# A list schedule that reaches from layer A to the last out projection, taken in passes from both ends

## The chip, the cores and the metric

The kernel runs on one core of a Trainium2 chip. The metric is the device time of one execution in microseconds (us), as the median over repeated executions. The profile and the trace come from one further execution on the hardware. Engines are named as the profile names them: PE (matmuls), PEld (its weight loads), DVE (vector), ACT (scalar), POOL (GpSimd) and SP, whose queue issues every DMA of this kernel.

## What is computed

One inference step of two layers, for a prompt of 1024 tokens and 8 samples of 8 tokens each (64 further columns), at width 1024. The reference, cut to what matters:

```python
def short_conv_mixer(u, buf, w_in, w_conv, w_out):          # layer A
    p = u @ w_in                                            # 1024 -> 4096
    y, new_buf = causal_dwconv(c_gate * h, buf, w_conv)
    return (b_gate * y * jax.nn.silu(z)) @ w_out, new_buf

def gdn_mixer(u, conv_buf, s0, w_in, w_conv, ...):          # layer B, 8 heads of 128
    p = u @ w_in                                            # 1024 -> 4112
    qkv, new_buf = causal_dwconv(p[..., :3072], conv_buf, w_conv)
    ...
    o, S = gated_delta_rule(q, k, v, g, beta, s0)           # triangular solve per chunk, scan over chunks
    o = o * lax.rsqrt(jnp.mean(o * o, ...) + NORM_EPS) * norm_w
    return (o * jax.nn.silu(z)) @ w_out, new_buf, S

for l in range(2):
    u = x * (1.0 + scale) + shift                           # shift, scale, gate = silu(c) @ w_mod + b_mod
    out, ... = mixer(u, ...)
    x = layer_norm(ALPHA * x + gate * out, ln_g[l], ln_b[l])
```

Activations and weights are float32.

## The kernel before

**Layer A.** The input of the layer is held as two fp32r tiles per column group, `uh` (rounded) and `ul` (the rest), in three groups of 384, 384 and 320 columns; every weight block is split the same way into `wh` and `wl` (ACT rounds, DVE subtracts). A product is three matmuls per 128 rows of k: `wh*uh`, `wh*ul`, `wl*uh` (`mm_k`). `chan_a(j)` computes channel block j from four such products; it ends with a multiplication on POOL and a store to the scratch tensor `d_y[0]`. Beside channels 1 and 2 the second layer's modulation (`mod_gate`, `mod_cols`, matmuls against `csT`) is computed, beside channels 3 to 7 the out-projection weights are split (`load_wo`).

**Out projection of a layer** (`out_proj`). Nine tiles of 128 tokens (the ninth has the 64 sample rows). Per tile: reload `y` from scratch and split it (`load_y`), 48 matmuls of 512 columns into two PSUM banks (`mm`), then `norm`: gate and residual on DVE, `bn_stats`, a square root on ACT, a Newton step on DVE, and `finish`. In layer A `finish_a` normalizes on ACT (`xt`), multiplies `x1` by the layer norm's vectors on POOL (two instructions of 1024 columns), transposes `xt` on PE into the bank `t1`, and forms `uh` and `ul` of layer B. In layer B `finish_b` ends in the store of `y`.

**Layer B.** 32 products of the same kind as in layer A (three per head and the gates `z`), and beside them per head and half a chain: `prep` (transposes, Gram products, then a triangular inverse by levels in fp16, tiles `AH`, `DH`, `EH`, `YH`, `id16`), `scan` (fp32 matmuls of 128 columns, `S` to `S`), and `norm_out`. `sample(p)` does the same for the samples of two heads; its last part updates the sample states `S0` (load, scale on ACT, one matmul of 512 columns, add on DVE, store). `out_weights` loads and splits layer B's out-projection weights into the space of `uh` and `ul` once the last products have read it.

**What sets the order.** Every instruction goes through `Clock`, which hands it to `Plan.add`. While `Plan.on` is true, `Plan` records it with a price (`Plan.price`: busy time, and the time until it is seen) and with the instructions that it depends on. `Plan.arrange` is a list scheduler: each of five queues (T is PE, V is DVE, A is ACT, G is POOL, D is SP's DMAs) takes, when it is free, the ready unit with the highest rank, and the order found is tied to the program by dependencies that cost no wait. Outside of it instructions stand as they are written. In the kernel before `Plan.on` is set ahead of `gates` (the start of layer B) and `arrange` is called behind the last chain, ahead of layer B's out projection; the rank is the longest way to the end of that stretch.

Of the kernel before, what the change touches and what calls it, by code (L numbers as in the profile page):

```python
# [8 lines left out]
F32R = mybir.dt.float32r  # L9
F16 = mybir.dt.float16  # L10
# [105 lines left out]
class Plan:  # L116
# [2 lines left out]


    CELL = 128
    on = False

    @classmethod
# [26 lines left out]
        return t  # L151


    V = ((1, 0.155), (128, 0.345), (256, 0.41), (512, 0.69), (1112, 1.34))
    G = ((1, 0.25), (128, 0.4), (512, 1.3), (1112, 2.65))

    @staticmethod
    def along(table, n):
# [5 lines left out]
    @classmethod  # L164
    def price(cls, kind, name, outs, ins, args, kw):
        n = outs[0].free_size()
        if kind == "T":
            x = kw["rhs"] if "rhs" in kw else None
            if x is None:
                return max(0.055, outs[0].free_size() * 0.00083 + 0.0025), 0.2  # L170
            n, cols = x.free_size(), kw["lhsT"].free_size()
            if x.dtype == F32R:
                return n * 0.0004475 + 0.0025, 0.2
            if x.dtype == F32:
                return max(0.222 if cols > 64 else 0.0, n * (2 / 1200.0 if cols > 32 else 0.5 / 1200.0) + 0.005), 0.2
            return max(0.029, n / 2400.0 + 0.0023), 0.2
        if kind == "D":
            return 0.06, 2.0 + min(x.free_size() for x in outs + ins) * P * 4 / 3e5
        if kind == "V":
            wide = [x for x in outs + ins if x.free_size() > 1]  # L180
            if len(wide) > 1 and all(x.dtype == F16 for x in wide):
                n = n / 2
            return cls.along(cls.V, n) - 0.08, 0.115
        if kind == "G":
            t = 1.02 if ALU.pow in args else cls.along(cls.G, n) * (1.0 if len(ins) > 1 else 0.5)
            return t - 0.06, 0.1
        t = 0.2 + 0.00066 * n if ins[0].space == PSUM else 0.18 + 0.0009 * n
        t += 0.2 * ("accum_out" in kw) + 0.11 * hasattr(kw.get("scale"), "free_size")
        return t - 0.1, 0.135


# [14 lines left out]
    @classmethod  # L206
    def add(cls, kind, name, outs, ins, args, kw, inst):
        if not cls.on:
            return
        i = len(cls.nodes)  # L210
        deps, behind = set(), set()
        bank = {x.name for x in (*ins, *outs) if x.space == PSUM}
        for x in bank:

            if x in cls.writer:
                j = cls.writer[x]
                (behind if cls.nodes[j][0] == kind else deps).add(j)
            cls.writer[x] = i
        rc = {c for x in ins if x.name not in bank for c in cls.cells(x)}
        wc = {c for x in outs if x.name not in bank for c in cls.cells(x)}  # L220
        for c in rc | wc:
            if c in cls.writer:
                deps.add(cls.writer[c])
        for c in wc:
            deps |= cls.readers.pop(c, set())
            cls.writer[c] = i
        for c in rc:
            cls.readers.setdefault(c, set()).add(i)
        for x in (*outs, *ins):
# [12 lines left out]
        if kind == "T":  # L242
            x = kw.get("rhs", kw.get("in_"))
            wide = x.dtype == F32R
            if cls.unit and cls.unit[1] == outs[0].name and not (wide and cls.unit[2] >= 3) and max(deps, default=0) < cls.unit[0]:
                unit = cls.unit[0]
                cls.unit[2] += 1
            else:
                cls.unit = [i, outs[0].name, 1]
        else:  # L250
            wide = False
            if cls.unit and any(x.name == cls.unit[1] for x in (*outs, *ins)):
                cls.unit = None
        func = args[2] if kind == "A" and len(args) > 2 else None
        table = {AF.Exp: 1, AF.Silu: 2, AF.Sqrt: 3}.get(func, 0)
        cls.nodes.append((kind, inst, unit, deps, *cls.price(kind, name, outs, ins, args, kw), wide, table, behind, [x.name for x in outs]))


    @classmethod
    def arrange(cls, tc):  # L260
        import heapq

        cls.on = False

        def order(i, j):
            tc.add_manual_dep(i, j.name, mybir.DependencyInfo(mybir.DependencyClass.NoSync, mybir.DependencyReason.DATA), reason="order")

        nodes = cls.nodes
# [1 line left out]
        for i, v in enumerate(nodes):  # L270
            units.setdefault(v[2], []).append(i)

            old = [d for x in v[9] for y in cls.before.get(x, ()) for d in cls.users.get(y, ())]
            deps.setdefault(v[2], set()).update(nodes[d][2] for d in (*v[3], *old))
            behind.setdefault(v[2], set()).update(nodes[d][2] for d in v[8])
            for d in v[8]:
                if nodes[d][0] != v[0]:
                    order(v[1], nodes[d][1])
        after, follow = ({u: [] for u in units} for _ in range(2))
        for u in units:  # L280
            deps[u].discard(u)
            behind[u] -= deps[u] | {u}
            for d in deps[u]:
                after[d].append(u)
            for d in behind[u]:
                follow[d].append(u)
        cost = {u: (sum(nodes[i][4] for i in units[u]), max(nodes[i][5] for i in units[u])) for u in units}
        left = {u: len(deps[u]) + len(behind[u]) for u in units}
        line = [u for u in units if not left[u]]
        for u in line:  # L290
            for v in after[u] + follow[u]:
                left[v] -= 1
                if not left[v]:
                    line.append(v)
        assert len(line) == len(units)
        way = {}
        for u in reversed(line):
            way[u] = max(sum(cost[u]) + max((way[v] for v in after[u]), default=0.0), max((way[v] for v in follow[u]), default=0.0))
        left = {u: len(deps[u]) + len(behind[u]) for u in units}
        ready = dict.fromkeys(units, 0.0)  # L300
        coming, waiting = ({k: [] for k in "TVAGD"} for _ in range(2))
        free, last = dict.fromkeys("TVAGD", 0.0), dict.fromkeys("TVAGD", None)
        state = {"T": True, "A": 0}
        for u in units:
            if not left[u]:
                heapq.heappush(coming[nodes[u][0]], (0.0, u))
        for _ in units:
            t, k = min((free[k] if waiting[k] else max(free[k], coming[k][0][0]), k) for k in "TVAGD" if waiting[k] or coming[k])
            while coming[k] and coming[k][0][0] <= t:
                u = heapq.heappop(coming[k])[1]  # L310
                heapq.heappush(waiting[k], (-way[u], u))
            u = heapq.heappop(waiting[k])[1]
            busy, seen = cost[u]
            if k == "T":
                wide = nodes[u][6]
                busy += 0.078 * (wide and not state["T"])
                state["T"] = wide
            elif k == "A" and nodes[u][7]:
                busy += 1.28 * (nodes[u][7] != state["A"])
                state["A"] = nodes[u][7]  # L320
            free[k] = t + busy
            for i in units[u]:
                if last[k] is not None:
                    order(nodes[i][1], last[k])
                last[k] = nodes[i][1]
            for v, at in [(v, t + busy + seen) for v in after[u]] + [(v, t) for v in follow[u]]:
                ready[v] = max(ready[v], at)
                left[v] -= 1
                if not left[v]:
                    heapq.heappush(coming[nodes[v][0]], (ready[v], v))  # L330


class Pool:
# [30 lines left out]
def tile_trunk(ctx, tc, I, O):  # L364
# [239 lines left out]
    with ExitStack() as actx:  # L604
# [270 lines left out]
                load_wm(9 + i)  # L875

        extra.extend(lambda i=i: mod_next(i) for i in range(len(mods)))
        load_wm(8)
        chan_a(1)
        chan_a(2)  # L880
# [87 lines left out]
    with ExitStack() as bctx:  # L968
# [15 lines left out]
        gt = ExitStack()  # L984
        gtp = pool_in(gt, "gt", 1)

        Plan.on = True

        def gates():
            cong = gtp.tile([P, const_width("cong")], F32, name="cong")  # L990
# [600 lines left out]
        while chains or filler or fillers or upcoming or todo:  # L1591
# [16 lines left out]
            else:  # L1608
# [3 lines left out]
                except StopIteration:  # L1612
                    filler = None
                drain(1)
        Plan.arrange(tc)
        sB2.close()
        sB.close()

# [11 lines left out]
        with ExitStack() as fctx:  # L1630
# [22 lines left out]

            out_proj(1, wk, (3, 2, 0), wo, gP, gS, finish_b, lns, beside, constants)
            beside(("sampled", 3))


_OUT = (("y_p", (SEQ, D)), ("y_s", (NS, D)), ("ca_p", (P, KT, 2)), ("cb_p", (P, 24, 3)), ("s_p", (H, P, P)),
# [100 lines left out]
```

## Time and profile before

| | |
|---|---|
| Median of 3 runs | 1360.61 us (1359.68 to 1361.13) |
| The profiled execution, own time | 1356.89 us |
| Its span | 1355.1 us |
| PE busy | 1309.0 us, 97% of the span |
| DVE, ACT, POOL busy | 831.9, 652.9, 209.4 us |
| DMA moved | 160.22 MB, 118 GB/s over the span |

The page divides the span into 40 slices and gives each engine's busy share in tenths. Matmuls are pipelined, so a PE that is busy throughout may still start its matmuls further apart than it could. All instructions stand on one line (L106), since `Clock` issues them all; groups are told apart by the tiles they write and read. Layer A runs to about 432 us, its out projection to about 558 us, layer B to about 1250 us, and its out projection to the end.

### The profile page before, as it was taken

Reading aid. Unit: us, or ns where it says so; the run is one execution under the profiler, and the core shown is the slowest. Engines: PE = TensorE matmul, PEld = TensorE weight load, DVE = VectorE, ACT = ScalarE, POOL = GpSimd, SP = SyncE. Lnnn points to the kernel's source line nnn. Section 1 sums busy time; section 2 is a strip of 40 time slices with the busy share of each in tenths; the row PEclk is TensorE's granted clock in tenths of the full one; section 3 lists DMA queues with packets and bytes.
Section 4 is the critical chain, followed back from the end, with each engine's and each line's share of the span. In section 5 each row is a group of like instructions: output and inputs, shape, how many; then the busy total and the mean of one; then the engine's idle time right before and its main releaser. Section 6 shows DMA issues by size and latency. Waiting matters only on the chain.

```text
span 1355.1 us, 27508 instructions
## 1 busy us (share of the span) xinstructions
PE 1309.0 (97%) x10631; PEld 1197.4 (88%) x10631; DVE 831.9 (61%) x2010; ACT 652.9 (48%) x1878; POOL 209.4 (15%) x326
## 2 busy tenths in 40 slices
PE   7999999999999999898999999999999999998997
PEld 5898889999999777798999899999999899996775
DVE  3444143244233688667866877787787667557687
ACT  3411212222221355478965768676776567445321
POOL 0011000000000144211121212130303102001041
PEclk9999999999999999999999999999999999999999
DMA  8735542221212332246331232222222224336852
GB/s 310 265 126 190 223 135 77 87 83 68 86 65 68 123 125 88 73 130 187 118 101 50 67 111 80 67 74 88 67 84 83 89 71 129 113 130 202 252 177 68
DMA packets 119023, 160.22 MB, mean 118 GB/s; under 512 B 21220, under 2 KB 74220, under 8 KB 116844
## 3 DMA queue, kind: packets, MB, share of 16 engines
q1 hardware_dynamic: 118892, 158.46, 36.3%
q8 instruction: 83, 1.36, 0.4%
q14 instruction: 48, 0.39, 0.1%
HBM read 123.61 MB, written 34.82 MB: 117 GB/s over the span
## 4 chain that ended last, share of the span: by engine, by line
PE 44%; DVE 7%; DMA 4%; ACT 2%; issue 1%; POOL 1%; SPq 0%; POOLq 0%; ACTq 0%; DVEq 0%
PE g L106 24%; PE t L106 13%; PE s L106 5%; PE o L106 3%; DVE acc L106 1%; DMA S<-in_s_dram 1%; DVE xt L106 1%; DVE wl L106 1%; DMA E<-d_rows 1%; DMA rb<-d_rows 1%; DMA wr<-in_wb_dram 0%; DMA wr<-d_y 0%; DVE Y L106 0%; POOL f1y L106 0%; DVE st L106 0%
## 5 line engine op out<-in xcount | busy, mean ns | idle before, releaser
L106 PE MATMUL g<-uh,wh 128*128 128x384 f32 (+3 forms) x1080 | 376.2, 352 | 1.1 <-DVE wh L106 0.8
L106 PE MATMUL g<-ul,wh 128*128 128x384 f32 (+3 forms) x1080 | 355.1, 332 | 0.0
L106 PE MATMUL g<-uh,wl 128*128 128x384 f32 (+2 forms) x1064 | 350.6, 333 | 0.2 <-DVE wl L106 0.2
L106 DVE TENSOR_TENSOR wl<-wr,wh 128x256 fp32r<-128x256 f32 (+1 forms) x225 | 133.6, 610 | 178.1 <-ACT wh L106 177.9
L106 ACT ACTIVATE wh<-wr 128x256 fp32r<-128x256 f32 (+2 forms) x227 | 109.3, 501 | 213.6 <-PE t L106 118.1
L106 PEld LDWEIGHTS g<-uh,wh 128*128 128x128 f32 (+1 forms) x1080 | 202.2, 187 | 6.1 <-issue 1.2
L106 PEld LDWEIGHTS g<-ul,wh 128*128 128x128 f32 (+1 forms) x1080 | 202.1, 187 | 2.8
L106 PEld LDWEIGHTS g<-uh,wl 128*128 128x128 f32 x1064 | 199.4, 188 | 2.7 <-DVE wl L106 0.5
L106 PE MATMUL t<-uh,wh 128*128 128x384 f32 (+3 forms) x540 | 177.7, 336 | 4.1 <-ACT uh L106 2.9
L106 PE MATMUL t<-ul,wh 128*128 128x384 f32 (+3 forms) x540 | 177.1, 335 | 0.1
L106 PE MATMUL t<-uh,wl 128*128 128x384 f32 (+2 forms) x532 | 173.7, 333 | 0.3 <-DVE wl L106 0.3
L106 DVE SCALAR_TENSOR_TENSOR acc<-xb,wbc,acc 128x512 f32<-128x512 f32 (+1 forms) x144 | 113.8, 792 | 19.1 <-ACT acc L106 18.5
L106 PEld LDWEIGHTS t<-uh,wh 128*128 128x128 f32 (+1 forms) x540 | 101.4, 188 | 16.0 <-issue 6.3
L106 PEld LDWEIGHTS t<-ul,wh 128*128 128x128 f32 (+1 forms) x540 | 101.8, 188 | 5.1 <-issue 2.1
L106 PEld LDWEIGHTS t<-uh,wl 128*128 128x128 f32 x532 | 100.3, 189 | 3.6 <-issue 0.8
L106 ACT ACTIVATE xb<-g 128x384 f32<-128x384 f32 (+4 forms) x122 | 49.7, 413 | 78.8 <-PE g L106 77.7
L106 ACT ACTIVATE EH<-t 128x256 f16<-128x256 f32 (+1 forms) x176 | 57.0, 365 | 5.4 <-PE t L106 4.7
L106 ACT ACTIVATE DH<-t 128x256 f16<-128x256 f32 (+1 forms) x128 | 46.6, 384 | 23.3 <-PE t L106 22.3
L106 PE MATMUL t<-DH,AH 128*128 128x64 f16 x1176 | 52.3, 193 | 1.5 <-DVE DH L106 0.9
L106 PEld LDWEIGHTS <-AH 128*128 128x128 f16 x1176 | 43.4, 98 | 9.9 <-issue 7.2
L106 PEld LDWEIGHTS <-EH 128*128 128x128 f16 x1120 | 41.9, 98 | 9.6 <-issue 4.3
L106 ACT ACTIVATE YH<-Y 128x256 f16<-128x256 f32 (+1 forms) x104 | 41.7, 402 | 17.1 <-DVE Y L106 15.2
(361 smaller groups left out, 2377.7 us busy)
## 6 DMA issues: line engine op xcount, KB each, us to landing
wm<-in_wm_dram SPq DMA_DIRECT2D x16, 1024.0 KB
wr<-in_wb_dram SPq DMA_DIRECT2D x64, 256.0 KB
wr<-in_wa_dram SPq DMA_DIRECT2D x62, 256.0 KB
wm<-in_wm_dram SPq DMA_DIRECT2D x16, 512.0 KB
wr<-d_y SPq DMA_DIRECT2D x32, 256.0 KB
S<-in_s_dram SPq DMA_DIRECT2D x32, 256.0 KB
d_y<-cs SPq DMA_DIRECT2D x8, 544.0 KB
wr<-in_wo_dram SPq DMA_DIRECT2D x16, 256.0 KB
```

Source lines behind the costliest of these rows:

```text
L106: r = call(*args, **kw)
```

## The change

The list schedule covers everything from channel 1 of layer A to the last instruction: `Plan.on` is set ahead of `load_wm(8)`, and `arrange` is called at the end. The scheduler itself is replaced. `order` is one pass of list scheduling over a graph; `arrange` runs six times forward and, between them, on the reversed graph, and each pass takes its ranks from the start times of the pass before; the forward pass with the smallest modelled end is used. On the PE queue a pass may stay with the kind of matmul that runs (fp16 or not) as long as the best of that kind is within `STAY` of the best of all, and it adds 0.08 when it leaves fp16. Prices change too: short DVE and POOL instructions cost a little more, `bn_stats` has its own price, and DMAs occupy their queue by size and run length instead of 0.06 each. What is computed stays the same, and so does each instruction; only places in the queues change.

```diff
+    STAY = 4.0
+    PASSES = 6
...
-    V = ((1, 0.155), (128, 0.345), (256, 0.41), (512, 0.69), (1112, 1.34))
-    G = ((1, 0.25), (128, 0.4), (512, 1.3), (1112, 2.65))
+    V = ((1, 0.18), (128, 0.345), (256, 0.41), (512, 0.69), (1112, 1.34))
+    G = ((1, 0.3), (128, 0.4), (512, 1.3), (1112, 2.65))
...
         if kind == "D":
-            return 0.06, 2.0 + min(x.free_size() for x in outs + ins) * P * 4 / 3e5
+
+            size = min(x.shape[0] * x.free_size() for x in outs + ins) * 4
+            run = min((x.ap[-1][1] if x.ap[-1][0] == 1 else 1) for x in outs + ins) * 4
+            rate = 340e3 if run >= 2048 else 300e3 if run >= 1024 else 200e3 if run >= 512 else max(8e3, run * 300.0)
+            return max(0.06, size / rate), 2.0
+        if kind == "V" and name == "bn_stats":
+            return 0.05 + 0.00106 * ins[0].free_size(), 0.115
...
-            wide = x.dtype == F32R
-            if cls.unit and cls.unit[1] == outs[0].name and not (wide and cls.unit[2] >= 3) and max(deps, default=0) < cls.unit[0]:
+            wide = 2 if x.dtype == F32R else x.dtype != F16
+            if cls.unit and cls.unit[1] == outs[0].name and not (wide == 2 and cls.unit[2] >= 3) and max(deps, default=0) < cls.unit[0]:
...
+    def order(cls, kinds, cost, edges, rank):
...
+        for _ in cost:
+            t, k = min((free[k] if waiting[k] else max(free[k], coming[k][0][0]), k) for k in "TVAGD" if waiting[k] or coming[k])
+            w = waiting[k]
+            while coming[k] and coming[k][0][0] <= t:
+                u = heapq.heappop(coming[k])[1]
+                heapq.heappush(w, (-rank[u], u))
+            top = w[0]
+            if k == "T":
+                if (kinds[top[1]][1] == 0) != (state[k] == 0):
+                    top = min((x for x in w if (kinds[x[1]][1] == 0) == (state[k] == 0) and x[0] <= top[0] + cls.STAY), default=top)
+                if kinds[top[1]][1] and not state[k]:
+                    t += 0.08
+                state[k] = kinds[top[1]][1]
+            elif k == "A" and kinds[top[1]][2]:
+                t += 1.28 * (kinds[top[1]][2] != state[k])
+                state[k] = kinds[top[1]][2]
...
+            u = top[1]
+            start[u], free[k] = t, t + cost[u][0]
+            queue[k].append(u)
+            for v, lag in edges[u]:
+                ready[v] = max(ready[v], t + lag)
...
+        return max(start[u] + sum(cost[u]) for u in cost), start, queue
...
         for u in reversed(line):
-            way[u] = max(sum(cost[u]) + max((way[v] for v in after[u]), default=0.0), max((way[v] for v in follow[u]), default=0.0))
...
+            rank[u] = max((rank[v] + lag for v, lag in ahead[u]), default=sum(cost[u]))
+        best = None
+        for _ in range(cls.PASSES):
+            r = cls.order(kinds, cost, ahead, rank)
+            if best is None or r[0] < best[0]:
+                best = r
+            start = cls.order(kinds, cost, back, {u: t + cost[u][0] for u, t in r[1].items()})[1]
+            rank = {u: t + cost[u][0] for u, t in start.items()}
+        for queue in best[2].values():
+            line = [i for u in queue for i in units[u]]
+            for i, j in zip(line, line[1:]):
+                tie(nodes[j][1], nodes[i][1])
...
+        Plan.on = True
         load_wm(8)
         chan_a(1)
...
-        Plan.on = True
-
         def gates():
...
-        Plan.arrange(tc)
         sB2.close()
         sB.close()
...
             beside(("sampled", 3))
+            Plan.arrange(tc)
```

Three places show what moves.

PE in layer B, inside `prep` of head 0: `t1` and `t0` are the banks of the two halves' level products, `g` the bank of a product with `uh` and `ul`. Before, the end of one fp16 group of the second half:

```order
L106 MATMUL t1_6282<-id16_76,DH1_5817 128x64
L106 LDWEIGHTS DH1_5817
L106 MATMUL t1_6282<-id16_76,DH1_5817 128x64
L106 LDWEIGHTS DH1_5817
L106 MATMUL t1_6282<-id16_76,DH1_5817 128x64
L106 MATMUL g_6445<-uh2_101,wh_5930 128x320
L106 MATMUL g_6445<-ul2_104,wh_5930 128x320
L106 MATMUL g_6445<-uh2_101,wl_5931 128x320
```

In the change, the end of the same group:

```order
L106 MATMUL t1_6282<-id16_76,DH1_5817 128x64
L106 LDWEIGHTS DH1_5817
L106 MATMUL t1_6282<-id16_76,DH1_5817 128x64
L106 LDWEIGHTS DH1_5817
L106 MATMUL t1_6282<-id16_76,DH1_5817 128x64
L106 LDWEIGHTS AH0_5724
L106 MATMUL t0_6325<-DH0_5725,AH0_5724 128x64
```

The fp16 group of the first half (`t0_6325`), which stood by itself between two pieces of a product before, now follows the second half's group. Over the whole program fp16 matmuls are followed by a matmul of another kind at 236 places before and at 151 places in the change.

PE in layer A's out projection, where the eight transposes of the second token tile (`xt_4003`) stand; its sums are complete with the last matmul into `t0_3857` and `t0_3858`. Before, they stand amid the products of the fourth tile (`g_4119`, `g_4120`):

```order
L106 MATMUL g_4119<-woh3_1800,wl_4007 128x512
L106 MATMUL g_4120<-woh3_1800,wl_4007 128x512
L106 MATMUL g_4119<-woh4_1802,wh_4012 128x512
L106 MATMUL t1_4093<-cons_75,xt_4003 128x128 x4
L106 MATMUL t1_4105<-cons_75,xt_4003 128x128 x4
L106 MATMUL g_4120<-woh4_1802,wh_4012 128x512
L106 MATMUL g_4119<-wol4_1803,wh_4012 128x512
L106 MATMUL g_4120<-wol4_1803,wh_4012 128x512
```

In the change they stand behind the last of them:

```order
L106 MATMUL g_4120<-woh6_1806,wl_4013 128x512
L106 MATMUL g_4120<-woh7_1808,wh_4012 128x512
L106 MATMUL g_4120<-wol7_1809,wh_4012 128x512
L106 MATMUL g_4120<-woh7_1808,wl_4013 128x512
L106 MATMUL t1_4093<-cons_75,xt_4003 128x128 x4
L106 MATMUL t1_4105<-cons_75,xt_4003 128x128 x4
L106 MATMUL t0_4235<-woh0_1794,wh_4170 128x512
L106 MATMUL t0_4235<-wol0_1795,wh_4170 128x512
```

Counted in matmuls from a tile's last product to its transposes: before, 51, 49 and five times 48 of 512 columns for the first seven tiles, and 24 of 512 and 24 of 256 for the eighth; in the change 48 for the first tile, 93, 96, 96 and 96 for the second to the fifth, 72 for the sixth, 72 and 39 of 256 for the seventh, 24 and 48 of 256 for the eighth. Behind the ninth stand 32 matmuls of 384 columns before and 27 in the change. On ACT, the first tile's square root and normalization stand ahead of three roundings (`wh_3972`, `wh_4006`, `wh_4012`) in the change and behind them before.

DVE at the end, behind the last products of the ninth tile's bank `g_17623` (`xt_17589` is the ninth tile, `xt_17497` the eighth, `S0` the last two sample states). Before:

```order
L106 TENSOR_TENSOR tmp_17736<-g_17623,gS_16817 64x256
L106 SCALAR_TENSOR_TENSOR xt_17589<-xt_17589,tmp_17736 64x256
L106 BN_STATS st_17723<-xt_17589 64x6
L106 BN_AGGR mv_17724<-st_17723 64x2
L106 TENSOR_SCALAR ve_17725<-mv_17724 64x1
L106 SCALAR_TENSOR_TENSOR xt_17589<-xt_17589,mv_17724,ln_g_16818 64x896
L106 RECIPROCAL rs_17742<-rt_17743 64x1
```

In the change:

```order
L106 TENSOR_TENSOR tmp_17736<-g_17623,gS_16817 64x256
L106 RECIPROCAL rs_17686<-rt_17687 128x1
L106 TENSOR_TENSOR S0_16944<-S0_16944,t0_16995 128x512
L106 SCALAR_TENSOR_TENSOR xt_17589<-xt_17589,tmp_17736 64x256
L106 TENSOR_TENSOR rt_17687<-rs_17686,ve_17674 128x1
L106 BN_STATS st_17723<-xt_17589 64x6
L106 SCALAR_TENSOR_TENSOR rt_17687<-rt_17687,rs_17686 128x1
L106 TENSOR_TENSOR S0_17014<-S0_17014,t0_17067 128x512
L106 BN_AGGR mv_17724<-st_17723 64x2
L106 SCALAR_TENSOR_TENSOR rs_17686<-rt_17687,rs_17686 128x1
L106 TENSOR_SCALAR ve_17725<-mv_17724 64x1
L106 TENSOR_SCALAR nm_17675<-mv_17673,rs_17686 128x1
```

The two additions into `S0`, whose matmuls are now the last two of the program on PE, and the end of the eighth tile stand between the ninth tile's instructions; before, they came earlier.

## Rows read from the trace of the kernel before

**Rows 1.** The page: busy time by engine.

```profile
PE 1309.0 (97%) x10631; PEld 1197.4 (88%) x10631; DVE 831.9 (61%) x2010; ACT 652.9 (48%) x1878; POOL 209.4 (15%) x326
```

**Rows 2.** Stages: busy us (instructions) of each engine, TensorE clock, DMA share, GB/s.

```profile
core 0: us, PE busy (x) PEld busy (x) DVE busy (x) ACT busy (x) POOL busy (x), PEclk, DMA share, GB/s
55.00:440.00 385.00, 385.00 (x2347) 367.22 (x2344) 136.43 (x293) 78.60 (x136) 25.70 (x36) 1.00 0.33 113
440.00:562.00 122.00, 112.50 (x539) 87.78 (x538) 93.37 (x160) 56.15 (x120) 42.79 (x23) 0.97 0.33 107
562.00:660.00 98.00, 93.65 (x722) 89.44 (x720) 71.80 (x196) 77.46 (x182) 11.72 (x32) 1.00 0.48 146
660.00:1200.00 540.00, 532.85 (x5866) 505.41 (x5866) 395.46 (x1042) 367.25 (x1246) 101.06 (x196) 1.00 0.28 85
1200.00:1355.10 155.10, 138.25 (x865) 112.99 (x863) 111.76 (x259) 51.28 (x147) 27.08 (x30) 0.97 0.56 174
```

**Rows 3.** Who PE waited for, 440 to 562 us: us, times, longest.

```profile
PE t L106 <- ACT xt L106: 7.2, 4, 2.8
PE t L106 <- ACT uh L106: 1.4, 1, 1.4
```

**Rows 4.** The same, 562 to 660 us.

```profile
PE t L106 <- DVE kn L106: 1.0, 1, 1.0
```

**Rows 5.** The same, 660 to 1200 us.

```profile
PE t L106 <- DMA S<-in_s_dram: 2.0, 2, 1.6
```

**Rows 6.** The same, 1200 us to the end.

```profile
PE s L106 <- DVE qg L106: 2.9, 1, 2.9
PE t L106 <- DMA S<-in_s_dram: 1.9, 1, 1.9
PE t L106 <- ACT wh L106: 1.1, 1, 1.1
```

**Rows 7.** Three short stretches, columns as in rows 2.

```profile
496.90:500.20 3.30, 3.30 (x11) 2.71 (x10) 3.30 (x2) 3.28 (x9) 3.22 (x2) 0.50 0.06 16
500.30:503.70 3.40, 3.40 (x16) 2.72 (x16) 3.40 (x4) 0.68 (x2) 1.17 (x1) 1.00 0.45 147
1251.20:1254.60 3.40, 3.40 (x11) 2.75 (x9) 2.08 (x4) 1.91 (x5) 0.00 (x0) 0.50 0.53 171
```

**Rows 8.** Timeline of PE behind a run of fp16 matmuls: start, us.

```profile
803.24 0.42 PE L106 MATMUL g<-uh,wh 128*128 128x384 f32 x1
803.50 0.34 PE L106 MATMUL g<-ul,wh 128*128 128x384 f32 x1
803.67 0.34 PE L106 MATMUL g<-uh,wl 128*128 128x384 f32 x1
```

**Rows 9.** Chain that ended last, two late pieces: start, us, what.

```profile
1312.45 11.04 PE g L106 x48
...
1342.81 2.81 PE g L106 x24
```

**Rows 10.** Timeline of DVE and POOL, 461 to 468 us.

```profile
461.12 0.69 DVE L106 TENSOR_TENSOR wl<-wr,wh 128x512 fp32r<-128x512 f32 x1
466.15 2.20 DVE L106 TENSOR_TENSOR wl<-wr,wh 128x512 fp32r<-128x512 f32 x1
465.39 2.40 POOL L106 TENSOR_TENSOR x<-xt,ln_g 128x1024 f32<-128x1024 f32 x1 [30.62 <-ACT rt L106]
```

**Rows 11.** Timeline of DVE, pieces of the last 100 us.

```profile
1257.90 0.69 DVE L106 TENSOR_TENSOR S<-S,t 128x512 f32<-128x512 f32 x1 [4.14 <-PE t L106]
1340.20 1.01 DVE L106 SCALAR_TENSOR_TENSOR xt<-xt,rs,ln_b 128x768 f32<-128x768 f32 x1
1348.61 0.15 DVE L106 TENSOR_TENSOR rt<-rs,ve 64x1 f32<-64x1 f32 x1
```

**Rows 12.** Timeline of SP and ACT: one load of out-projection weights.

```profile
1239.71 0.34 SPq L106 DMA_DIRECT2D xb<-in_wo_dram  x1
1243.36 1.15 ACT L106 ACTIVATE uh<-xb 128x512 fp32r<-128x512 f32 x2 [0.78 <-DMA xb<-in_wo_dram]
```

More of the change, by code (lines that the diff above doesn't have):

```diff
@@ L187, in price @@
         t = 0.2 + 0.00066 * n if ins[0].space == PSUM else 0.18 + 0.0009 * n
-        t += 0.2 * ("accum_out" in kw) + 0.11 * hasattr(kw.get("scale"), "free_size")
+        t += 0.2 * ("accum_out" in kw) + 0.1 * hasattr(kw.get("scale"), "free_size")
         return t - 0.1, 0.135
@@ L259, in arrange, with tie @@
     @classmethod
+    def order(cls, kinds, cost, edges, rank):
+        import heapq
+        left, ready = dict.fromkeys(cost, 0), dict.fromkeys(cost, 0.0)
+        for u in cost:
+            for v, _ in edges[u]:
+                left[v] += 1
+        coming, waiting = ({k: [] for k in "TVAGD"} for _ in range(2))
+        free, state, queue, start = dict.fromkeys("TVAGD", 0.0), {"T": 2, "A": 0}, {k: [] for k in "TVAGD"}, {}
+        for u in cost:
+            if not left[u]:
+                heapq.heappush(coming[kinds[u][0]], (0.0, u))
+        for _ in cost:
[14 more added lines that the diff above has]
+                state[k] = kinds[top[1]][2]
+            if top is w[0]:
+                heapq.heappop(w)
+            else:
+                w.remove(top)
+                heapq.heapify(w)
+            u = top[1]
[3 more added lines that the diff above has]
+                ready[v] = max(ready[v], t + lag)
+                left[v] -= 1
+                if not left[v]:
+                    heapq.heappush(coming[kinds[v][0]], (ready[v], v))
+        return max(start[u] + sum(cost[u]) for u in cost), start, queue
+    @classmethod
     def arrange(cls, tc):
-        import heapq
         cls.on = False
-        def order(i, j):
+        def tie(i, j):
             tc.add_manual_dep(i, j.name, mybir.DependencyInfo(mybir.DependencyClass.NoSync, mybir.DependencyReason.DATA), reason="order")
@@ L277, in arrange @@
                 if nodes[d][0] != v[0]:
-                    order(v[1], nodes[d][1])
-        after, follow = ({u: [] for u in units} for _ in range(2))
+                    tie(v[1], nodes[d][1])
+        kinds = {u: (nodes[u][0], nodes[u][6], nodes[u][7]) for u in units}
+        cost = {u: (sum(nodes[i][4] for i in units[u]), max(nodes[i][5] for i in units[u])) for u in units}
+        ahead, back = ({u: [] for u in units} for _ in range(2))
         for u in units:
[L281 to L288, printed above, removed]
+            lags = {d: 0.0 for d in behind[u]}
+            lags.update((d, sum(cost[d])) for d in deps[u])
+            lags.pop(u, None)
+            for d, lag in lags.items():
+                ahead[d].append((u, lag))
+                back[u].append((d, cost[u][0] + lag - cost[d][0]))
+        rank = {}
+        left = {u: len(back[u]) for u in units}
         line = [u for u in units if not left[u]]
         for u in line:
-            for v in after[u] + follow[u]:
+            for v, _ in ahead[u]:
                 left[v] -= 1
@@ L295, in arrange @@
         assert len(line) == len(units)
-        way = {}
         for u in reversed(line):
-            way[u] = max(sum(cost[u]) + max((way[v] for v in after[u]), default=0.0), max((way[v] for v in follow[u]), default=0.0))
[L299 to L330, printed above, removed]
```

## The prediction

> **What bounds the kernel now.** I read the busy line of the page first: PE is busy for 97% of the span, DVE for 61%, ACT for 48% [rows 1]. So time can only come from PE: from places where it waits, and from places where it starts its matmuls further apart than it must. Next I cut the span into stages [rows 2]. From 55 to 440 us (layer A's channels) PE is busy in all 385 us, and no row of the waits names it there: the schedule cannot gain in the larger part of the stretch that it newly covers. From 440 to 562 us (layer A's out projection) PE is idle for 122.0 - 112.5 = 9.5 us, from 562 to 660 us (the start of layer B) for 4.4, from 660 to 1200 us for 7.2 of 540, and from 1200 us to the end for 16.9, of which 9.5 lie behind the last matmul, which ends at 1342.81 + 2.81 = 1345.6 [rows 9]. That is 38 us of idle PE in all. Then I read the waits of PE stage by stage: in the out projection the transposes wait four times for the normalized tile, 7.2 us together, and the last gate product 1.4 us for `uh` [rows 3]; at the start of layer B the chain's first steps wait, as for `kn`, 1.0 us at a time [rows 4]; in the body the longest total is 2.0 us for a sample state's load [rows 5]; around 1250 us there are 2.9, 1.9 and 1.1 us [rows 6].
>
> Two further costs do not show as idle time. The granted clock fell from its 2.4 GHz level to 1.2 GHz (0.50 in the rows) in three stretches of some 3.3 us, each right behind a wait of PE: 11 matmuls start in 3.3 us, and 16 in the 3.4 us that follow [rows 7], so each such stretch costs about 5 matmuls of 0.23 us, 1.2 us. And behind a run of fp16 matmuls the next product starts its second matmul after 0.26 us, where the following distance is 0.17 [rows 8]: leaving fp16 costs 0.08 to 0.09 us.
>
> **The change part by part.** Nothing is added or removed; PE's work is the same, so each term is a wait or a change of kind that appears or goes. The sum is made against the profiled span of 1355.1 us; that execution took 1356.89 us, 3.7 below the median of 1360.61, and I carry the difference over to the median.
>
> (a) Fewer exits from fp16. 236 exits become 151: 85 x 0.08 = -6.8 us. This counts in full only where PE is the bound, and in the body it is: 7.2 us idle in 540. Bounds -7.2 and 0 (a chain that now waits for its partner could give it back).
>
> (b) Layer A's out projection. The wait in front of the transposes is what the norm needs, less what stands between. Before, 51 matmuls of 0.23 us [rows 9] stood there and PE still waited 2.8 us, so the first tile's norm took 51 x 0.23 + 2.8 = 14.5 us. Now the second to the seventh tile have at least 72 matmuls, 16.6 us, in between: their waits go. The first has 48 (11.0 us), but its norm goes ahead of three roundings on ACT, 0.6 us each [rows 12], and of the splits on DVE; I expect a wait of 0 to 1.5 us. The eighth had 24 of 512 and 24 of 256 columns, now 24 and 48 (some 11 us in place of 8). The ninth has fewer than before, so the 1.4 us behind it stay. Of 7.2 us I take 5.8 as gone, and of the two slow-clock stretches of this stage the one behind a transposes' wait: 5.8 + 1.2 = -7. Bounds -8.4 and 0.
>
> Here one observation speaks against the change. DVE's split of a tile takes 0.69 us, but 2.20 us when it begins while POOL multiplies `x1` [rows 10]. The Trainium skill says why (SBUF — State Buffer, Who interferes with whom): a DVE instruction with both inputs in SBUF and a GpSimd instruction that reads SBUF take the same read interface, and whichever comes second waits until the other ends. The trace agrees, with 2.20 against 0.69 us. By that rule the planner's prices are wrong here, since they give such a DVE instruction one price whatever POOL does. In the sum it stays out, because the same 18 POOL instructions run in either order; it is the slower rival below.
>
> (c) Start of layer B. The first transposes of `kn`, the first Gram products and the first fp16 steps stand 1 to 5 us of products later than before, which covers waits of 1.0 us each [rows 4]. Idle time was 4.4 us: -2.5. Bounds -4.4 and +2 (the gates' chain decides, and nobody fills more).
>
> (d) Body of layer B. The waits are of eight kinds, none over 2.0 us in total [rows 5]; the new order is made by the same kind of list, so I expect as many in other places: 0, bounds -5 and +6.
>
> (e) Around 1250 us. The chain of the last head and the final sample states met there. Now the products reach about 10 us further into the last scan, and the last sample states are put off to the end, so the waits for `qg` and for the state's load shrink. A new one comes: on SP the load of the second block of out-projection weights stands behind the store of the last head's state, and a load takes 3.65 us from its issue to the rounding that uses it [rows 12]; PE has 18 matmuls of the first block, 4.1 us, to run meanwhile, part of them already behind it; I count 1 to 2 us of wait. Of 5.9 us [rows 6] and one slow-clock stretch of 1.2 us I take -5. Bounds -7.1 and +3.
>
> (f) The end. DVE works off the ninth tile's norm behind the last matmul. Now two additions into the sample states, 0.69 us each, one instruction of 768 columns, 1.01 us, and some six short ones of 0.15 us [rows 11] stand between: 1.4 + 1.0 + 0.9 = +3.3. Bounds 0 and +4.
>
> (g) Layer A's channels: there was no wait, so a new order can only add one. The modulation is done earlier, with its weights loaded closer together. +1, bounds 0 and +3 (one wait of the longest kind in these rows, 2.9).
>
> Sum: -6.8 - 7 - 2.5 + 0 - 5 + 3.3 + 1 = -17. The span becomes 1338, the median 1360.6 - 17 = **1343.6 us**.
>
> **The rivals.**
>
> *Given back in part.* The waits move on instead of going: the first tile still waits, each stage keeps half of its waits, and the fp16 steps, now tied in pairs, wait for the slower half. For it: idle time of PE is small and spread, and ACT is busy for 77.46 us of 98 at the start of layer B [rows 2]. Against it: the distances in the out projection grew from 12 to over 16 us. Then (a) -4, (b) -3.5, (c) and (e) -3 together, (f) and (g) +4.3: -6, about 1354 us.
>
> *No change.* What was gained in the body is lost at the end and in the newly planned channels, or the order of instructions does not do what its model says because DMA decides: within 2.7 us of 1360.6. For it: the end is longer by 3.3 us for sure, and layer A's channels can only lose.
>
> *Slower: DVE is held by POOL in layer A's out projection.* This is the rule named above, as a mechanism of this kernel: a planned DVE order that places instructions with two SBUF inputs under the POOL pair of each tile. DVE is busy for 93.37 of 122 us there [rows 2], with nine tiles 10.4 us a tile; PE needs 48 x 0.23 and the transposes, about 11.9 us a tile. Each further instruction caught costs 2.20 - 0.69 = 1.5 us, so from the second one a tile on, DVE is the bound. With four more, 10.4 + 6.0 - 11.9 = 4.5 us are lost on each of seven tiles, 32 us, and (b) is not earned: -10 + 32 = +22, about 1382 us; with three more, +11. Against it: the POOL pair takes about 5 us a tile, before as now, and PE's transposes now stand a full tile later, so that a late DVE has room first.
>
> **How the numbers follow.** Forecast (-10 to -27 us) 0.60; given back in part (-2.7 to -10) 0.21; no change 0.09; slower 0.10, nearly all of it the POOL mechanism with three or more instructions a tile. A difference of 0.2%, 2.7 us, is about what a measurement of this kernel can tell from none. So faster 0.81, same 0.09, slower 0.10. The range: all best bounds of (a) to (g) together give -32, which is too much to expect; -30 is the low end, 1330. The high end takes in the partial return and the lower half of no change: 1358. Outside remain the slower case and a little on either side.
>
> **What would show it.** In the profile of the changed kernel: of PE's waits between 440 and 562 us the one for `xt` falls from 7.2 to under 2 us, and only one or no slow-clock stretch lies there; between 660 and 1200 us PE's work takes some 7 us less; around 1250 us the wait for `qg` is under 1 us, and a wait for `uh` or `wl` behind a weight load takes its place; behind the last matmul 12 to 13 us pass instead of 9.5, with `S` among DVE's last instructions. The prediction is wrong if layer A's channels show PE idle, if the out projection lasts as long as before with DVE busy throughout, or if the body's waits grow by more than the 6.8 us that the exits give.

## The result, and the profile after

The changed kernel takes 1337.20 us (median of 4 runs, 1334.88 to 1338.62) against 1360.14 us (4 runs) of the kernel before: ratio 0.9831, 95% interval [0.9813, 0.9849], 22.9 us less. On a second chip it again took 1337.19 us, but the kernel before took 1353.79 there: ratio 0.9865 [0.9843, 0.9886], 16.6 us less. The change repeats itself; the kernel before moves by some 6 us from chip to chip. The forecast of 1343.6 us lies 6.4 us above the result and inside its range. The profiled execution has a span of 1335.9 us against 1355.1. So the two traces show 19.2 of the 22.9 us between the medians; the other 3.7 come from which executions were profiled, 3.25 us below its median before (1356.89 us) and 0.4 above it in the change (1337.63).

The busy line of the page, which answers to [rows 1]: the same work, PE still at 97% of a span that is 19.2 us shorter.

```profile
PE 1296.5 (97%) x10631; PEld 1193.8 (89%) x10631; DVE 834.3 (62%) x2010; ACT 656.3 (49%) x1884; POOL 207.3 (16%) x326
```

The stages, columns as in [rows 2]:

```profile
55.00:440.00 385.00, 382.79 (x2345) 365.01 (x2344) 134.70 (x291) 73.23 (x136) 30.01 (x37) 1.00 0.33 110
440.00:562.00 122.00, 115.40 (x550) 90.60 (x549) 97.49 (x167) 57.14 (x124) 42.53 (x22) 0.96 0.37 117
562.00:660.00 98.00, 96.28 (x764) 94.36 (x763) 68.56 (x185) 78.92 (x180) 12.24 (x34) 0.99 0.41 131
660.00:1200.00 540.00, 535.95 (x6056) 512.47 (x6055) 411.74 (x1100) 383.92 (x1296) 96.99 (x200) 1.00 0.30 91
1200.00:1335.90 135.90, 119.59 (x632) 96.60 (x630) 99.09 (x208) 40.93 (x103) 24.51 (x26) 0.97 0.59 187
```

Idle PE is now 2.2 us in layer A's channels (0 before), 6.6 in its out projection (9.5), 1.7 at the start of layer B (4.4), 4.1 in the body (7.2) and 16.3 behind 1200 us (16.9). Whom PE waited for, the same five stretches in order:

```profile
PE g L106 <- DVE xb L106: 1.1, 1, 1.1
PE t L106 <- DVE cs L106: 1.1, 1, 1.1
...
PE s L106 <- ACT wh L106: 3.4, 1, 3.4
PE t L106 <- ACT xt L106: 2.0, 1, 2.0
PE t L106 <- ACT uh L106: 0.6, 1, 0.6
...
PE t L106 <- DVE kn L106: 1.7, 1, 1.7
...
PE t L106 <- DVE DH L106: 1.2, 2, 0.6
PE s L106 <- DVE vn L106: 0.9, 1, 0.9
...
PE s L106 <- DVE wl L106: 2.5, 1, 2.5
PE s L106 <- DVE qg L106: 1.6, 1, 1.6
PE t L106 <- ACT vx L106: 1.4, 1, 1.4
```

Against [rows 3]: `xt` fell from 7.2 us in four waits to one of 2.0 (the ninth tile's), but a wait of 3.4 us for `wh` is new, and the granted clock falls behind both. Columns as in [rows 7]:

```profile
467.60:471.00 3.40, 3.40 (x10) 2.65 (x9) 0.69 (x1) 3.21 (x9) 0.00 (x0) 0.50 0.90 284
471.00:474.40 3.40, 3.40 (x16) 2.73 (x15) 3.06 (x4) 0.95 (x2) 1.68 (x1) 1.00 0.07 29
556.30:563.10 6.80, 5.95 (x24) 4.07 (x24) 3.95 (x9) 3.23 (x9) 2.88 (x9) 0.50 0.25 63
```

The stretch at the 1.2 GHz level near 560 us is 6.8 us long now; before it was about 3.4. These two cost much of the gain in this stage: layer A's last product ends 2.5 us later than before, the out projection's last one 3.3 us earlier, and the last gate product at the same time, 562.2 us.

At the end, pieces of the chain that ended last (start, us, what):

```profile
1320.31 2.80 PE g L106 x24
1323.11 0.25 PE t L106
...
1325.30 0.69 DVE S L106
...
1326.45 0.93 DVE xt L106
...
1327.45 1.46 DVE xt L106
```

The last product ends at 1323.11 us, 22.5 us earlier than in [rows 9]; behind it 12.75 us pass instead of 9.50.

**Where the time came from**, in the two traces, each stage from the end of one's last product to the end of the next. A pause here is more than 0.25 us beyond the usual distance of such matmuls:

| | predicted | measured |
|---|---|---|
| (a) exits from fp16, 236 and 151 | -6.8 | -6.75 (19.25 to 12.5 us) |
| (b) layer A's out projection and gates | -7 | -2.4 |
| (c) to 660 us, pauses | -2.5 | -3.8 (5.75 to 1.9) |
| (d) body, pauses | 0 | -4.75 (10.8 to 6.0) |
| (e) from 1200 us, pauses | -5 | -3.9 (8.8 to 4.95), and some of the next row |
| smaller distances and low clock in (c) to (e) | | -3.3 |
| (f) the end | +3.3 | +3.25 |
| (g) layer A's channels | +1 | +2.5 |
| sum | -17 | -19.2 |

The sum and the ends of stages do not depend on how a pause is counted, the split between the rows does: with the usual distance taken from the matmul in front, (a) is 17.6 to 11.1 us, (c) 5.4 to 1.9, (d) 9.3 to 5.2 and (e) 8.7 to 4.7.

### The profile page after: what moved, and what is told of

Read it like the earlier page. It is cut to its first block, busy times and chain, and to the rows that moved or that the text cites. A ratio compares the mean times of both kernels' runs of the same rounds, so it can differ in the third digit from the quotient of the medians.

```text
span 1335.9 us, 27510 instructions
## 1 busy us (share of the span) xinstructions
PE 1296.5 (97%) x10631; PEld 1193.8 (89%) x10631; DVE 834.3 (62%) x2010; ACT 656.3 (49%) x1884; POOL 207.3 (16%) x326
## 5 line engine op out<-in xcount | busy, mean ns | idle before, releaser
L106 PE MATMUL g<-uh,wh 128*128 128x384 f32 (+3 forms) x1080 | 382.6, 356 | 1.5 <-DVE xb L106 1.1
L106 DVE TENSOR_TENSOR wl<-wr,wh 128x256 fp32r<-128x256 f32 (+1 forms) x225 | 139.0, 630 | 59.3 <-ACT wh L106 58.9
L106 DVE COPY bias<-t 128x1 f32<-128x1 f32 x29 | 4.6, 157 | 148.2 <-PE t L106 148.2
L106 DVE TENSOR_TENSOR Y<-t,cons 128x256 f32<-128x256 f32 (+1 forms) x104 | 41.5, 404 | 21.1 <-PE t L106 20.7
```

The source lines that it names most:

```text
L106: r = call(*args, **kw)
```

## The experiments

All ratios are to the kernel before on the same chip; "the change" is 0.9831 or 0.9865 by chip, as above.

| run | us | ratio, 95% interval |
|---|---|---|
| e1_new_list_old_stretch | 1340.09 | 0.9885 [0.9866, 0.9904] |
| e2_old_list_new_stretch | 1377.33 | 1.0158 [1.0137, 1.0179] |
| e3_no_stay | 1341.64 | 0.9897 [0.9878, 0.9916] |
| e4_one_pass | 1340.36 | 0.9890 [0.9871, 0.9910] |
| e5_change_again | 1337.19 | 0.9865 [0.9843, 0.9886] |
| e6_small_steps | 1331.34 | 0.9823 [0.9801, 0.9845] |
| e7_states_earlier | 1339.04 | 0.9879 [0.9857, 0.9900] |
| e8_both_mends | 1332.93 | 0.9832 [0.9811, 0.9854] |
| e9_old_list_new_prices | 1348.50 | 0.9931 [0.9913, 0.9949] |
| e10_new_list_old_prices | 1368.51 | 1.0075 [1.0053, 1.0098] |
| e11_old_dma_price | 1369.08 | 1.0086 [1.0067, 1.0104] |
| e12_before_small_steps | 1356.53 | 0.9988 [0.9975, 1.0001] |

**One part of the change at a time.** First the new scheduler and prices where the old ones stood:

```diff
-        Plan.on = True
         load_wm(8)
...
+        Plan.on = True
         def gates():
...
+        Plan.arrange(tc)
         sB2.close()
```

> The new scheduler and prices on the old stretch (layer B's main part alone); 158 exits from fp16 instead of 236, layer B's end and both out projections in the old order. Theory (each exit costs 0.08 us, and the other gain comes from covering layer B's end together with its out projection): 78 x 0.08 = 6.2 us and a few us of waits in the body, so 1350 to 1354 us; waits around 1250 us and the end of 9.5 us as before the change. Rival (the new ranks take the waits away wherever they are): 1340 to 1346 us.

The rival's range held: 1340.1 us. Layer A's out projection stands as before, with its waits for `xt` of 7.2 us, and yet nearly the whole gain is there. What the larger stretch adds is small: 2.9 us by the medians, which are from different chips; by the ratios 0.2 or 0.54%, 2.7 or 7.3 us, as the second or the first chip's value of the change is taken, and only the second one's interval overlaps. The run has the new scheduler and the new prices together, so it does not tell which of the two earns this over the old stretch.

Then the opposite, the old scheduler and the old prices over the larger stretch (`Plan.on` ahead of `load_wm(8)` and `arrange` at the end, all else as before the change):

> The old scheduler and prices on the new stretch; 232 exits. Theory: no gain from exits, some 8 us from layer B's end, 3 us lost behind the last matmul (the last two state updates are the last matmuls here too), so 1352 to 1357 us. Rival (covering more is the whole gain): 1337 to 1343 us. Second rival (the old ranks, made for one end, spoil layer A): over 1360 us.

It is slower than before, by 1.6%. That lies in the second rival's range, but its mechanism is not there: to the last gate product the run loses only 3.4 us, but its last layer B product ends 20.4 us late, and PE then waits once for 10.1 us in the last out projection:

```profile
PE g L106 <- DVE tmp L106: 10.1, 1, 10.1
```

So the larger coverage by itself does not explain the gain. Two small edits of the new scheduler follow, on the same chip as these two: `STAY = 0.0`, and `PASSES = 1`.

> The change with STAY = 0: 237 exits instead of 151, layer B's end and the last matmuls in the same places. Theory: 86 x 0.08 = 6.9 us more than the change, 1343 to 1345 us. Rival (pairing makes chains wait, so that without it waits go down): 1335 to 1340 us.

> The change with PASSES = 1: ranks from the longest way alone; 173 exits. Theory: 22 x 0.08 = 1.8 us more, 1338 to 1340 us, since the last product and the last scan stand in the same places. Rival (the passes from both ends carry the gain): 1345 us or more.

Without staying, 237 matmuls leave fp16. In the trace, from 562 us on, that costs 19.4 us against 12.5 in the change, the 6.9 us expected, while pauses are alike (12.8 and 12.9). The time is 4.4 us over the change's by the medians. One pass leaves 173 exits and costs 3.2 us (both against medians of other chips). The first lies 1.4 us below its theory's range and the second 0.4 above, and neither is the missing cause.

**Prices or scheduler.** Two runs fill the square: the old scheduler with the new prices, and the new one with the old prices.

```diff
-    V = ((1, 0.18), (128, 0.345), (256, 0.41), (512, 0.69), (1112, 1.34))
+    V = ((1, 0.155), (128, 0.345), (256, 0.41), (512, 0.69), (1112, 1.34))
...
-            return max(0.06, size / rate), 2.0
+            return 0.06, 2.0 + min(x.free_size() for x in outs + ins) * P * 4 / 3e5
```

(the second run's edit, cut; the first is the reverse, made on e2). A third changes the last of these lines alone.

> The scheduler of the kernel before (one pass, ranks by the longest way, no staying with fp16), over the changed kernel's stretch, with the changed kernel's prices. With the old prices this was 1377 us. Theory (the prices are what lets the larger stretch pay: DMAs that occupy their queue are issued in time for the last out projection): 1340 to 1352 us, and the 10.1 us wait of PE for DVE's tmp in the last out projection goes. Rival (passes, ranks and staying are what it needs): 1365 to 1380 us, with waits of the same kind.

> The changed kernel's scheduler over its stretch, with all prices as before the change. Theory (prices): 1352 us or more, with long waits of PE in the last out projection. Rival (passes, ranks and staying): 1334 to 1344 us, as the changed kernel. In between, both count.

> The changed kernel with the price of DMAs alone as before (0.06 each on the queue, later seen by size). Theory (of the prices it is this one that matters): the time is within 4 us of the run with all old prices. Rival (the short DVE and POOL prices matter, or none does): within 4 us of the changed kernel's 1337.

| over the larger stretch | old prices | new prices |
|---|---|---|
| old scheduler | 1377.3 | 1348.5 |
| new scheduler | 1368.5 | 1337.2 |

The prices are worth 29 and 31 us, the scheduler 9 and 11, by medians of several chips between which the kernel before moves by 6 us. And the price of DMAs alone accounts for the prices: 1369.1 us with only that one undone. The price decides whether the larger stretch pays. Over the old stretch it was not tried by itself. Of the scheduler's 11 us at the new prices, exits are the larger part: the old scheduler leaves fp16 at 228 places there against 151, 77 x 0.08 = 6.2 us.

SP's queue in the run with the old DMA price (start, us, operation), then what PE and ACT waited for:

```profile
1260.39 0.32 SPq L106 DMA_DIRECT2D gP<-d_gate  x1
1260.76 0.43 SPq L106 DMA_DIRECT2D wr<-d_y  x1
1261.23 1.45 SPq L106 DMA_DIRECT2D xt<-d_x  x3
1262.72 0.44 SPq L106 DMA_DIRECT2D ln_g<-in_ln_g_dram  x1
1263.20 0.44 SPq L106 DMA_DIRECT2D xt<-d_x  x1
1263.69 1.36 SPq L106 DMA_DIRECT2D ln_b<-in_ln_b_dram  x1
1265.09 0.71 SPq L106 DMA_DIRECT2D xt<-d_x  x1
...
1270.04 12.62 SPq L106 DMA_DIRECT2D wr<-d_y  x2
...
1280.90 1.15 ACT L106 ACTIVATE wh<-wr 128x512 fp32r<-128x512 f32 x2 [18.67 <-DMA wr<-d_y]
...
1281.59 0.79 PE L106 MATMUL s<-uh,wh 128*128 128x512 f32 x1 [12.16 <-ACT wh L106]
```

At 0.06 us each the planner takes eight loads of 512 KB (`gP`, five `xt`, `ln_g`, `ln_b`) for half a microsecond of the queue, and puts them, and three loads of 256 KB for the samples (left out above), ahead of the 256 KB of `y` that the next tile needs. The eight alone are 4.2 MB and need some 14 us at the 304 GB/s that the profile shows between 1260 and 1270 us, and the `wr` load that SP issues first at 1270.04 is rounded at 1280.90. PE stands for 12.2 us. The run of the old scheduler with old prices has the same row (`xt` x3, `ln_g`, `xt`, `ln_b`, `xt`, and behind them `wr`); there DVE stands 13.7 us for the split of this `y`, and the `tmp` that PE waits for stands behind it. In the change, where the same load is priced at about 1.5 us:

```profile
1241.96 0.32 SPq L106 DMA_DIRECT2D gP<-d_gate  x1
1242.33 1.95 SPq L106 DMA_DIRECT2D wr<-d_y  x2
1244.33 0.98 SPq L106 DMA_DIRECT2D xt<-d_x  x2
1245.35 0.43 SPq L106 DMA_DIRECT2D ln_g<-in_ln_g_dram  x1
1249.17 1.26 SPq L106 DMA_DIRECT2D wr<-d_y  x2
1250.48 0.97 SPq L106 DMA_DIRECT2D xt<-d_x  x2
```

The `y` loads alternate with the others, and PE never waits that long. From the last layer B product to the last out projection product pass 106.6 us in the change, 108.2 with the old scheduler and new prices, and 130.2, 128.3 and 121.8 in the three runs with the old DMA price (that price alone undone, all prices with the new scheduler, all with the old one).

The long wait is not the whole price, though. The new scheduler with all old prices plans the same burst of loads (1263.93 to 1272.26 us), its longest wait of PE behind it is 5.0 us, and it is as slow. What the three have in common shows in two sums, up to the last product:

| | PE idle from 55 us on | at the 1.2 GHz level |
|---|---|---|
| the change | 18.8 | 10.2 |
| e9, old scheduler, new prices | 20.9 | 10.2 |
| e2, old scheduler, old prices | 42.6 | 30.7 |
| e10, new scheduler, old prices | 37.3 | 41.0 |
| e11, old DMA price alone | 41.8 | 37.5 |

With the same scheduler, the old prices bring 18 to 23 us more of idle PE and 20 to 31 us more at the low clock. The queue above shows where 12.2 us of the idle time come from in e11; the other waits were not traced one by one.

**The wait that is new.** In the change, around 460 us, DVE, POOL, ACT and PE:

```profile
459.90 0.16 DVE L106 RECIPROCAL rs<-rt 128x1 f32<-128x1 f32 x1 [0.27 <-ACT rt L106]
460.10 1.60 DVE L106 TENSOR_TENSOR rt<-rs,ve 128x1 f32<-128x1 f32 x1
461.73 0.16 DVE L106 SCALAR_TENSOR_TENSOR rt<-rt,rs 128x1 f32<-128x1 f32 x1
461.93 2.19 DVE L106 SCALAR_TENSOR_TENSOR rs<-rt,rs 128x1 f32<-128x1 f32 x1
...
459.28 2.40 POOL L106 TENSOR_TENSOR x<-xt,ln_g 128x1024 f32<-128x1024 f32 x1 [22.01 <-ACT xt L106]
461.75 2.35 POOL L106 TENSOR_TENSOR x<-x,ln_b 128x1024 f32<-128x1024 f32 x1
...
464.41 1.24 ACT L106 ACTIVATE xt<-xt,nm,rs 128x1024 f32<-128x1024 f32 x1 [4.54 <-DVE nm L106]
...
466.22 0.50 PE L106 MATMUL s<-woh,wh 128*128 128x512 f32 x1 [3.41 <-ACT wh L106]
```

Two steps of the second tile's norm, one number per partition each, take 1.60 and 2.19 us in place of 0.15 and 0.16: each ends when a POOL multiplication of the first tile ends. That is 3.5 us, the normalization on ACT is late by it, the rounding of `wh` stands behind it, and PE waits 3.41. The prediction named a rule of the Trainium skill for this (SBUF — State Buffer, Who interferes with whom): a DVE instruction with two inputs in SBUF contends with a GpSimd instruction that reads SBUF, and one with at most one such input does not, two-port modes aside. The rows agree: the reciprocal, with one input, took 0.16 us under the same POOL instruction. To test it, the second factor of these three steps was given as a per-partition scalar; every instruction keeps its place:

```diff
-            newton(rs, rt, ve[:n])
+            V.tensor_scalar(rt, rs, ve[:n], None, ALU.mult)
+            V.tensor_scalar(rt, rt, rs, -0.5, ALU.mult, ALU.mult)
+            V.tensor_scalar(rs, rt, 1.5, rs, ALU.add, ALU.mult)
```

> The changed kernel itself once more, so that the other runs of this chip, and those that leave out one part of it, have it beside them. Ratio to the kernel before 0.983, as at first. Theory on the waits: one wait of 3.4 us of PE for ACT's wh at the second tile of layer A's out projection, and 12.7 us behind the last product.

> Every instruction keeps its place on every engine; the three DVE instructions of the Newton step in the out projections take their second factor as a per-partition scalar instead of a second tile. Theory (POOL holds DVE): in the changed kernel two of these 128x1 instructions of the second tile took 1.60 and 2.19 us instead of 0.15, under the pair of POOL multiplications of the first tile; that is 3.5 us, and PE's wait of 3.4 us for wh, which stands behind this tile's normalization on ACT, is those 3.5 us. Then the wait goes to under 0.5 us, the low clock behind it goes too, and the time falls by 3.5 to 5 us against the changed kernel (ratio to the kernel before about 0.980). Rival (the order on ACT alone: wh stands too late whatever DVE does): the wait stays over 2.5 us and the time within 1.5 us. Third possibility: a scalar operand is held in the same way, the two instructions stay at 1.5 to 2.2 us and nothing changes.

```profile
459.62 0.21 DVE L106 TENSOR_SCALAR rt<-rs,ve 128x1 f32<-128x1 f32 x1
459.87 0.22 DVE L106 TENSOR_SCALAR rt<-rt,rs 128x1 f32<-128x1 f32 x1
460.12 0.21 DVE L106 TENSOR_SCALAR rs<-rt,rs 128x1 f32<-128x1 f32 x1
...
458.80 2.42 POOL L106 TENSOR_TENSOR x<-xt,ln_g 128x1024 f32<-128x1024 f32 x1 [22.08 <-ACT xt L106]
...
462.44 0.50 PE L106 MATMUL s<-woh,wh 128*128 128x512 f32 x1 [0.17 <-ACT wh L106]
```

The three steps pass under the same POOL instruction at full speed, PE's wait is 0.17 us, and no low clock follows. The last gate product ends 3.4 us earlier than in the change's run on this chip, and the median falls by 5.85 us, a little more than expected; the four runs of each do not overlap (1329.11 to 1332.92 against 1335.07 to 1337.90). Of the 5.85 the two traces show 3.4 in this stage; the rest I cannot place. (The traces are of the fastest of the change's four executions and the slowest of these four, with spans only 2.1 us apart.) **This version beats both kernels.**

The same three lines in the kernel before:

> The kernel before with the Newton step's second factor as a per-partition scalar, as in the run of the small steps. Two of these instructions took 2.37 and 2.17 us there, and PE waited 2.8 and 0.8 us for the normalized tiles behind them. Theory (POOL held them): those two waits fall to under 1 us together and the time falls by 2 to 4 us (ratio about 0.998). Rival (in the old order the products of the other tiles leave no room, the wait is taken over by the split that POOL held for 2.20 us): the time stays within 1.5 us.

1.2 us less, inside the rival's 1.5, but the interval (3.4 us less to 0.1 more) does not exclude the theory's 2. The waits for `xt` add up to 7.1 us as before, in six pieces instead of four, the first of them 2.9 us (2.8 before). This run's trace shows why the first one stays:

```profile
466.32 2.28 DVE L106 SCALAR_TENSOR_TENSOR xt<-xt,tmp 128x512 f32<-128x512 f32 x1
468.52 0.20 DVE L106 TENSOR_SCALAR rt<-rs,ve 128x1 f32<-128x1 f32 x1
468.65 2.77 DVE L106 TENSOR_TENSOR wl<-wr,wh 128x512 fp32r<-128x512 f32 x1
```

The small step takes 0.20 us, but the wide addition in front of it and the split behind it, about 0.7 us each when nothing holds them, take 2.28 and 2.77 us under POOL's pair (465.67 to 470.87 us). The wide instructions take the hold over, as the rival said.

**The end.** One price makes the last sample states' stores urgent, so that their updates move some 40 us ahead:

```diff
-            return max(0.06, size / rate), 2.0
+            return max(0.06, size / rate), 16.0 if ins[0].name.startswith("S0") else 2.0
```

> The changed kernel with one price altered: stores of the sample states count as seen 16 us later instead of 2, so the scheduler puts the last states' updates some 40 us ahead of the end instead of at it. Theory (the two additions into S0 and the short instructions at the end cost 3.3 us): the time behind the last product falls from 12.7 to 10 to 11.5 us, and the time by 1.5 to 3.5 us against the changed kernel. Rival (the ninth tile's own norm decides, as it is spread by other short instructions anyway): behind the last product 12 us or more, no difference over 1 us; or the updates cost as much PE wait where they stand now, around 1200 us.

> The two edits together: short instructions with a scalar operand, and the sample states earlier. If both theories hold they add up, 5 to 8 us below the changed kernel (ratio to the kernel before 0.977 to 0.979); if only one holds, its own gain.

Behind the last product 11.45 and 11.1 us pass, so 1.3 to 1.6 us of term (f) can be had back; but the time does not fall (1.85 us more than the change, 1.6 more than the small steps alone, intervals overlapping). In the profile of the first, the slowest of its five executions (1342.56 us), PE waits 2.0 us for the updates (`vx`) at 1242 us and 2.4 us for a split at 1317, both followed by low clock: there the updates cost PE about as much where they went, as the rival said. In the profile of the second the wait for `vx` is 1.3 us and no low clock lies behind it; why that kernel is not faster is not shown.

## Why the prediction was right, point by point

The sign, the size and the range held. Two terms were right to a few tenths: (a), exits at 0.08 us each, which the run without staying shows from the other side, and (f), the instructions counted on DVE behind the last product. (c) and (e) were near, and lay within their bounds. How close the sum came is in part luck, as (b) and (d) below show.

(b) was mis-sized, -7 against -2.4. The step that failed is "I expect a wait of 0 to 1.5 us" at the first tiles: it was 3.4, with a stretch of low clock behind it. The cause is the mechanism of my slower rival, and it struck not the wide splits I had counted with, which took 2.4 us on average where they began under POOL without PE waiting, but two steps of 0.15 us on the path of a norm. With it taken away (e6), the last gate product ends 4.6 us earlier than before in a run whose channels end 1.9 us later: -6.5 us for the stage, against my -7. What remains there are mainly the ninth tile's waits, 2.0 and 0.7 us, and 6.8 us at the 1.2 GHz level. (The prediction counts 18 POOL instructions in this stage; the traces have 16, two for each of eight tiles. Its sum does not use the number.)

(d) was mis-sized, 0 against -4.75. The step that failed is "the new order is made by the same kind of list, so I expect as many in other places". Scheduler and prices are both new, and in the body either alone lowers the waits. Idle PE between 660 and 1200 us is 7.2 us before; over the larger stretch it is 8.0 with the old scheduler and old prices, 4.9 with the old scheduler and new prices, 4.4 with the new scheduler and old prices, and 4.1 in the change. With the DMA price alone undone it is 7.0, which no simple sum of the two gives; which of them acts in the change stays open.

I had also named the new DMA price in the change and given it no term; I had counted on the order as it came out, in which its effect was contained, without asking what held that order up. With the old price the change would have been 0.9% slower than before, by a mechanism that none of my rivals priced (the one of no change says only "because DMA decides"): loads that the planner takes for free, ahead of one that a tile waits for. What kept the sum close is that (b) and (d) missed by 4.6 and 4.75 us in opposite directions. That is luck, though either miss alone would have left the time inside the range.

(g) was +2.5 against +1: two waits of 1.1 us each, from the channels' newly planned order, where I had expected one unknown wait. So one of my signs of a wrong prediction, idle PE in layer A's channels, came true at 2.2 us. I had set it too narrowly, since my own sum allowed for such a wait.

Of the other marks: the exits, the end and the additions into `S` came as said, and `xt` fell to 2.0 us, where I had said under 2. The wait for `qg` is 1.6 us, not under 1; a weight wait did appear (2.5 us for `wl`, though for the ninth tile's split at 1312 us and not for a weight load). Two low-clock stretches lie in layer A's out projection, not one or none.

## What to carry to other kernels

When a scheduler's reach is extended, ask first which resource its prices leave free of charge: over the larger stretch one DMA price was worth 31 us here and the scheduler 9 to 11, while the reach itself brought some 3 to 7. Read the planned queues for a burst of large loads ahead of a small one that is due. And look at the one-number instructions of a norm that run beside POOL: given their second factor as a scalar operand they cost 0.2 us, as a second tile up to 2.2.

## What was not expected of the hardware

A DVE instruction of one element per partition is held by a POOL multiplication like a wide one: 1.60 and 2.19 us instead of 0.15. The same arithmetic with the factor as a per-partition scalar is not held (0.21 to 0.22 us, three in a row under one POOL instruction). Not every pause of PE is followed by the low level of the clock: those of 3.4 us at 466 and 2.0 at 555 us were, one of 2.5 us at 1312 was not, nor in the kernel before the longest of [rows 3], 2.8 us. Near 560 us, where pauses of 0.6 and 0.3 us followed the first, the level stayed low for 6.8 us.
